# Hybrid decoder trunk, one core: the first quarter's scale on the chip instead of through DRAM, and the second quarter's embedding moved to the last heads

## The chip, the core and the metric

The kernel runs on one core of a Trainium2 chip. Its engines are TensorE (PE in the profile, with PEld for the loading of weights), VectorE (DVE), ScalarE (ACT), GpSimd (POOL) and SyncE (SP), which issues all the transfers of this kernel. Each engine works off its own instructions in order and waits on semaphores for the others. The metric is the device time of one execution in microseconds (us). Before the change the median of three runs was 2870.23 us (2867.57 to 2871.44); the profiled execution, which all the rows below come from, took 2865.62 us.

## What is computed

One layer over 2048 tokens of width 1024, in float32:

```python
hn   = rms_norm(x, pre_mix_norm)
proj = hn @ w_in                       # 1024 -> 32 blocks of 128, and 8 columns for decay and beta
o_a  = gated DeltaNet, 4 heads of 128  # short conv, l2norm, chunked delta rule, gated head norm
o_b  = HGRN2, 4 heads of 128           # lower-bounded forget gate, chunked, gated head norm
h    = x + rms_norm(concat(o_a, o_b) @ w_out, post_mix_norm)
y    = square(relu(rms_norm(h, pre_mlp_norm) @ w_mlp_up)) @ w_mlp_down     # width 4096
h    = h + rms_norm(y, post_mlp_norm)
e    = rms_norm(p @ w_ple_proj, ple_norm)                                  # p has width 256
out  = h + e * sigmoid(h @ w_ple_gate)
```

`rms_norm(x, w)` is `x * rsqrt(mean(x * x) + 1e-6) * w` over the 1024 columns of a token.

## The kernel before, in words

**Tiling.** The tokens are worked in four quarters of 512 (`QT`). Activations lie transposed, features on the 128 partitions and tokens along the free dimension, so a 1024-wide operand is eight tiles of 128x512. A matrix product splits each operand into a high and a low part (`split`: ACT rounds a copy to fp32r, VectorE subtracts), and takes three matmuls per 128 features: high by high, high by low, low by high. A block of 128 output columns over 1024 features is thus 24 matmuls of 128x512; an embedding tile, over the 256 features of p, is six.

**Stages.** A first stage (pool `es`) embeds quarters of p and prepares the first quarter of x. Then, for each quarter, the mixers: first `mm_ab`, the projection of the eight decay and beta columns, then four heads, each with eight projections (`works`, line 910 on). Last come the output projection, the MLP and the gated addition of e.

**Order.** The PE's instructions stand in the order in which the program writes them (`manual_schedule`); in the first stage and through the mixers this holds for SP too. On the other engines a scheduler orders the instructions by its own estimate of the time. The mixers use a clock of ticks: a projection of 24 matmuls is three ticks of eight, and generators such as `gdn_mixer`, `decays` and `norm_steps` are put into an agenda (`at`) so that each of their steps is issued at a given tick. An engine that waits holds up all that stands behind it in its queue, and this goes for SP's transfers too.

**The first stage (lines 349 to 396).** It loads the weights of the embedding (`plea0`, `plea1`), two quarters of p (`praw`), the first quarter of x by rows (`xs`, 2 MB), constants, and the first quarter of x transposed (`xraw`, 2 MB). ACT squares the rows of x with a sum per row; VectorE and POOL turn the sums into scales, four per partition. `spread` stores these to DRAM as a row and `spread_load` loads the row back to all partitions. `operand` then scales a tile of `xraw` and splits it into the ring pool `ra` (ten buffers). In between, sixteen calls of `embed_tile` embed the two quarters: six matmuls, a copy `e` by ACT that is stored to `ed`, a square by ACT, and an addition by VectorE into `acc_e`.

**The first head's chain.** After `mm_ab`, `decays` (line 448) computes the decays on ACT and VectorE, sums them with scans into `gb`, stores them (`gd`) and has PE transpose them (`ps_gb`). `gdn_mixer` loads them back (`gf_g`), forms a lower triangular matrix (`u_g`), stores and reloads it in another layout (`ud_g`, `sys_g`), and VectorE solves it in 31 steps of a product and a reduction (lines 615 and 616). The result goes through DRAM once more (`xd_g`, `xx_g`) and PE uses it from `psp_g` (line 638) on. The tiles `bound`, `um`, `S` and `gb` take over the room of the pool `es`, so their memsets wait for the last store of an `e`.

**The buffers of the weights.** In the pool `wp` (line 438 on) raw weights have two buffers and split ones three. A split weight is also stored to a DRAM cache (`keep`), so its buffer comes free only when PE has used it and that store has landed. Loads, splits and stores run two to three projections ahead.

**The last heads (lines 939 to 977).** When all projections are done, the mixers of the last head still have steps to run. Between these, the embeddings of the third and fourth quarter fill PE, one tile per tick (`fill`), and then the first two tiles of the output projection (`first_outs`, `mmo`). Their copies `e` use two buffers ("ld" of the pool `m2`), which the raw tiles of p share.

Of the kernel before, what the change touches and what calls it, by code (L numbers as in the profile page):

```python
# [77 lines left out]
def trunk(ctx, tc, x, xT, pT, vecs, w_in, w_ab, gdn_a_log, gdn_dt_bias, w_out, w_up, w_down,  # L78
# [39 lines left out]
    def col(r):  # L118
        return cols[:, r : r + 1]
# [10 lines left out]
    def vectors():  # L130

        ps = bank("ps_rows", pp)
        PE.transpose(ps[:, :N_ROWS], rows, ident[:N_ROWS, :N_ROWS])
        V.tensor_copy(cols, ps[:, :N_ROWS])
        V.tensor_scalar(gate_w, cols[:, R_GNORM : R_HNORM + 1], 0.5, None, ALU.mult)
# [141 lines left out]
    def stage_ple(i, name):  # L277
# [5 lines left out]
        def ready(eng):  # L283
            w = wp.tile([P, 2, KD, P], F32R, tag="whl", name=f"w_{name}")
            for half in range(2):
                sl = slice(half * KD // 2, (half + 1) * KD // 2)
                split(w[:, :, sl], eng, raw[:, sl])
            return w
# [15 lines left out]
    x_r, xts, accs = {}, {0: []}, {0: None, 1: None}  # L304
# [44 lines left out]
    with ExitStack() as ectx:  # L349
        es = ectx.enter_context(tc.tile_pool(name="es", bufs=1))  # L350
        with tc.manual_schedule(engines={mybir.EngineType.SP}):
            ple0 = stage_ple(0, "plea0")
            praw = [es.tile([P, 2, QT], F32, name=f"praw{q}") for q in range(2)]
            nc.sync.dma_start(praw[0], pT[:, tok(0)].rearrange("(k p) t -> p k t", p=P))
            rows4 = x[tok(0), :].rearrange("(p c) d -> p c d", c=NC)
            xs = es.tile([P, NC, D], F32, name="xs")
            for c in range(0, NC, 2):
                nc.sync.dma_start(xs[:, c : c + 2], rows4[:, c : c + 2])
            nc.sync.dma_start(ident, consts[:, C_IDENT])
            nc.sync.dma_start(rows, vecs)  # L360
            nc.sync.dma_start(dec[:, 0:1], gdn_a_log.rearrange("o h -> h o"))
            nc.sync.dma_start(dec[:, 1:2], gdn_dt_bias.rearrange("o h -> h o"))
            nc.sync.dma_start(praw[1], pT[:, tok(1)].rearrange("(k p) t -> p k t", p=P))
            ple1 = stage_ple(1, "plea1")
# [6 lines left out]
            ple = [ple0(V), None]  # L371
            pts = [[operand(ra, None, f"pT{q}_{k}", raw=praw[q][:, k]) for k in range(2)] for q in range(1)]
            ss = sm.tile([P, NC], F32, tag="ss", name="ss_x0")
            for c in range(NC):
                S.activation(xs[:, c], xs[:, c], AF.Square, accum_out=ss[:, c : c + 1])
            V.tensor_scalar(ss, ss, 1.0 / D, EPS, ALU.mult, ALU.add)
            rsqrt(ss)
            stores = []
            for d in range(4):
                stores.append(embed_tile(0, d, ple[0], pts[0], accs, es, 6))  # L380
                if d == 1:
                    vectors()
            pts.append([operand(ra, None, f"pT1_{k}", raw=praw[1][:, k]) for k in range(2)])
            ple[1] = ple1(V)
            x_r[0] = spread(ss, "x0")
            rsb = spread_load(x_r[0], "x0")
            for d, q in [(d, 1) for d in range(4)] + [(d, q) for d in range(4, KD) for q in range(2)]:
                stores.append(embed_tile(q, d, ple[d // 4], pts[q], accs, es, 6))
                stores.pop(0)()
                if len(xts[0]) < KD:  # L390
                    k = len(xts[0])
                    xts[0].append(operand(ra, None, f"xt0_{k}", col(R_PREMIX + k), rsb, raw=xraw[:, k]))
            for f in stores:
                f()


    with mixers as mctx:
# [36 lines left out]

        def stage(name, src, k=KD):

            raw = wp.tile([P, k, P], F32, tag="raw", name=f"raw_{name}", bufs=2)
            nc.sync.dma_start(raw, src)

            def ready():  # L440
                w = wp.tile([P, 2, k, P], F32R, tag="whl", name=f"w_{name}")
                split(w, V, raw)
                return w

            return ready
# [378 lines left out]
        staged, split_w = {}, {}  # L824
# [81 lines left out]
        for q in range(2):  # L906
            at(0, norm_steps(accs[q], 1.0 / D, EPS, f"e{q}", partial(ple_r.__setitem__, q)),
               [4 * q + i for i in (0, 2, 4, 5)])
        with tc.manual_schedule(engines={mybir.EngineType.SP}):
            stage_work(0)  # L910
            stage_work(1)
            split_work(0)
            stage_work(2)
            split_work(1)
            for j, (name, key, src, q, h, then, g, b) in enumerate(works):
# [9 lines left out]
                for s in range(SPT):  # L925
                    for i in range(s * nt // SPT, (s + 1) * nt // SPT):
                        PE.matmul(ps, *terms[i], start=i == 0, stop=i == nt - 1)  # L927
# [7 lines left out]
            qs = (2, 3)  # L935
            ple = [stage_ple(i, f"pleb{i}") for i in range(2)]
            pts = {q: [operand(ra, pT[blk(k), tok(q)], f"pT{q}_{k}", stage=m2) for k in range(2)] for q in qs}
# [3 lines left out]
            at(clock[0], mix_operands(0), (1, 2, 3, 4, 6, 7, 9, 11))  # L941
# [3 lines left out]
            call(clock[0] + 13, partial(ready_out, 1))  # L945
            call(clock[0] + 14, partial(stage_out, 2))
# [693 lines left out]
```

## Time and profile before

| | |
|---|---|
| median of three runs | 2870.23 us |
| the profiled execution, its span | 2865.62 us, 2863.8 us |
| PE, PEld busy | 97%, 80% |
| DVE, ACT, POOL busy | 75%, 46%, 4% |
| read from and written to HBM | 420.14 MB, 166.92 MB |
| first matmul of mm_ab | 46.09 us after the start |
| third tile of the output projection | from 1245.56 us |

In a row of the timeline the first number is the start and the second the time, in us; then engine, line of the kernel, operation, output <- inputs, shapes and count; in brackets stands the idle time of the engine ahead of it and who ended it. `SPq` is a transfer being issued, not its landing. In a group of the list by line stand the count, the busy time in us, the mean of one in ns, and the idle time before. A window lists the busy time of PE, PEld, DVE, ACT and POOL, the granted clock of PE as a share, the share of the DMA engines and GB/s.

### The profile page before, as it was taken

What the parts mean: (1) busy time and instruction counts of PE and PEld (TensorE: products, weight loads), DVE (VectorE), ACT (ScalarE), POOL (GpSimd) and SP (SyncE); (2) the same over time, 40 slices, a digit from 0 to 9 for tenths busy, and PEclk for the clock granted to TensorE, in tenths of its full rate; (3) what the DMA queues carried; (4) which work ended last, traced back from release to release, by engine and by line L of the source; (5) the groups of instructions that cost most, each with busy time, mean ns of one, the idle gap of its engine ahead of it and who ended that gap; (6) DMA issues with size and microseconds to landing.
All of it is one profiled execution on the core that took longest, in us unless ns stands there. A gap on an engine that the chain in (4) does not pass through costs nothing.

```text
span 2863.8 us, 39544 instructions
## 1 busy us (share of the span) xinstructions
PE 2773.0 (97%) x13361; PEld 2293.7 (80%) x13361; DVE 2158.2 (75%) x4712; ACT 1331.2 (46%) x2460; POOL 108.7 (4%) x104
## 2 busy tenths in 40 slices
PE   7899999999999999999989999999999999999999
PEld 5688788888888888777768887888888888887887
DVE  6688787887878887758887886776787765567675
ACT  6354334333333333457555655554555445465431
POOL 0000000000000000000000000000100000001000
PEclk9999999999999999999999999999999999999999
DMA  7666667655665666587755646666564446577573
GB/s 254 223 222 205 215 213 246 201 199 201 224 195 190 212 199 196 159 284 247 258 173 192 229 166 209 217 212 210 193 210 139 148 157 213 188 255 239 196 230 116
DMA packets 268602, 589.70 MB, mean 206 GB/s; under 512 B 55642, under 2 KB 59960, under 8 KB 249072
## 3 DMA queue, kind: packets, MB, share of 16 engines
q1 hardware_dynamic: 268400, 587.18, 61.5%
q8 instruction: 106, 1.74, 0.3%
q14 instruction: 96, 0.79, 0.1%
HBM read 420.14 MB, written 166.92 MB: 205 GB/s over the span
## 4 chain that ended last, share of the span: by engine, by line
PE 46%; DVE 3%; DMA 3%; issue 2%; ACT 2%; POOL 0%; SPq 0%; DVEq 0%; ACTq 0%; POOLq 0%
PE u L996 21%; PE d L996 18%; PE mmg L996 6%; DMA da<-sumd 1%; DMA raw_out<-in_w_out_dram 1%; DMA xo<-in_xT_dram 1%; DMA b<-h1d 0%; PE mmo L996 0%; DVE w_out L162 0%; DVE t L162 0%; ACT L1033 0%; ACT L1032 0%; ACT w_out L161 0%; DVE b L1143 0%; POOL acc_y L225 0%
## 5 line engine op out<-in xcount | busy, mean ns | idle before, releaser
L927 PE MATMUL mm<-xt,w 128*128 128x512 f32 x3072 | 791.2, 405 | 2.6 <-ACT w L161 1.2
L927 PEld LDWEIGHTS mm<-xt,w 128*128 128x128 f32 x3072 | 564.6, 191 | 122.8 <-ACT w L161 1.6
L996 PE MATMUL d<-db,da 128*128 128x512 f32 x2688 | 613.0, 390 | 4.2 <-DVE db L215 3.2
L996 PE MATMUL u<-t,wu 128*128 128x512 f32 x2604 | 603.4, 393 | 3.3 <-ACT wu L161 3.2
L996 PEld LDWEIGHTS d<-db,da 128*128 128x128 f32 x2688 | 504.0, 188 | 112.6 <-DVE db L215 5.8
L996 PEld LDWEIGHTS u<-t,wu 128*128 128x128 f32 x2604 | 488.8, 188 | 117.2 <-ACT wu L161 4.1
L215 DVE TENSOR_TENSOR db<-db 128x512 fp32r<-128x512 f32 x224 | 160.8, 718 | 69.9 <-ACT db L214 69.4
L1325 DVE TENSOR_TENSOR u<-u,u 128x512 f32<-128x512 f32 x224 | 150.8, 684 | 72.1 <-PE u L996 71.0
L996 PE MATMUL mmo<-mixT,w_out 128*128 128x512 f32 x720 | 171.5, 398 | 9.1 <-DVE w_out L162 6.8
L214 ACT ACTIVATE db<-db 128x512 fp32r<-128x512 f32 x224 | 140.9, 629 | 78.7 <-DMA db<-hid 76.3
L996 PE MATMUL mmg<-h2T,wg 128*128 128x512 f32 x768 | 177.5, 393 | 0.0
L996 PEld LDWEIGHTS mmo<-mixT,w_out 128*128 128x128 f32 x720 | 137.0, 191 | 42.6 <-DVE w_out L162 8.5
L996 PEld LDWEIGHTS mmg<-h2T,wg 128*128 128x128 f32 x768 | 144.2, 188 | 32.8
L1366 ACT ACTIVATE u<-u 128x512 f32<-128x512 f32 x128 | 80.9, 632 | 179.6 <-DVE u L1325 179.2
L162 DVE TENSOR_TENSOR da<-da 128x512 fp32r<-128x512 f32 x128 | 94.3, 737 | 91.0 <-ACT da L161 90.5
L615 DVE TENSOR_TENSOR pr_g<-xs_g,sys_g 128x4 f32<-128x4 f32 (+30 forms) x496 | 136.1, 274 | 29.3 <-DMA sys_g<-ud_g 19.3
L161 ACT ACTIVATE da<-da 128x512 fp32r<-128x512 f32 x128 | 80.5, 629 | 140.0 <-DMA da<-sumd 117.3
L616 DVE TENSOR_REDUCE xs_g<-pr_g 128x4 f32<-128x8 f32 (+30 forms) x496 | 111.0, 224 | 9.8
L161 ACT ACTIVATE wu<-a 128x512 fp32r<-128x512 f32 x124 | 73.9, 622 | 46.7 <-DMA a<-in_w_up_dram 44.6
L225 POOL TENSOR_TENSOR acc_y<-acc_y,sq_y 128x512 f32<-128x512 f32 x28 | 38.7, 1382 | 1389.4 <-ACT sq_y L224 1389.4
L162 DVE TENSOR_TENSOR wu<-a,wu 128x512 fp32r<-128x512 f32 x124 | 84.9, 688 | 4.0 <-ACT wu L161 4.0
L726 PE MATMUL at_h<-q_h,k_h 128*128 128x64 f32 x640 | 82.6, 273 | 3.2 <-DVE tail_g L548 1.7
(364 smaller groups left out, 3893.1 us busy)
## 6 DMA issues: line engine op xcount, KB each, us to landing
w<-cache_in SPq DMA_DIRECT2D x96, 1024.0 KB
db<-hid SPq DMA_DIRECT2D x224, 256.0 KB
cache_in<-w SPq DMA_DIRECT2D x32, 1024.0 KB
hid<-u SPq DMA_DIRECT2D x128, 256.0 KB
da<-sumd SPq DMA_DIRECT2D x128, 256.0 KB
a<-in_w_up_dram SPq DMA_DIRECT2D x124, 256.0 KB
hid<-ht SPq DMA_DIRECT2D x96, 256.0 KB
dr<-in_w_down_dram SPq DMA_DIRECT2D x96, 256.0 KB
```

Of the source, the lines that this page charges most:

```text
L161: S.activation(t[:, 0], raw, AF.Copy)
L162: eng.tensor_tensor(t[:, 1], raw, t[:, 0], ALU.subtract)
L214: S.activation(t[:, 0], plain(t), AF.Copy)
L215: V.tensor_tensor(t[:, 1], plain(t), t[:, 0], ALU.subtract)
L225: eng.tensor_tensor(acc, acc, sq, ALU.add)
L615: V.tensor_tensor(pr[:, :, 0:i], xs[:, :, 0:i], sys[:, None, 0:i, i].broadcast_to([P, GC, i]), ALU.mult)
L616: V.tensor_reduce(xs[:, :, i], pr[:, :, 0 : i + 1], AX.X, ALU.add)
L726: PE.matmul(ps[:, c, :], k[:, blk(c)], odd, start=True, stop=True)
L927: PE.matmul(ps, *terms[i], start=i == 0, stop=i == nt - 1)
L996: PE.matmul(ps, a, b, start=start, stop=stop)
L1325: V.tensor_tensor(c[new], c[old], ps, ALU.add)
L1366: S.activation(c[k], c[k], AF.Relu)
```

## The change

In the first stage the rows of x are no longer loaded. ACT squares the transposed tiles two at a time and VectorE adds them up; four matmuls of one column each sum over the partitions, with the tokens on the partitions of the result. The scales, four per partition as before, multiply the identity matrix into a diagonal, and one matmul with all ones gives the row of scales on all partitions, in PSUM (`rs_x0`), where the scaling of x reads it. ACT and VectorE now follow the written order in this stage, as SP does: scalings run one tile ahead of the splits, and copies of embedding tiles stand at chosen places between them. The first two weights of the projections are loaded and the first is split here as well (`stage` is moved up unchanged). The e tiles are stored after the scalings, their squares are kept in pairs and added at the end, followed by `vectors()`.

Only the first quarter of p is embedded here. The second joins the third and fourth in the last heads, so `fill` has 24 tiles; p of a later quarter is loaded when the seventh tile of the quarter before is issued. The ticks of the output projection's first operands and weights, of the first norm of e and of the first decays' transposes are moved.

```diff
@@ first stage
-        with tc.manual_schedule(engines={mybir.EngineType.SP}):
+        first = {mybir.EngineType.SP, mybir.EngineType.Activation, mybir.EngineType.DVE}
+        with tc.manual_schedule(engines=first):
             ple0 = stage_ple(0, "plea0")
-            praw = [es.tile([P, 2, QT], F32, name=f"praw{q}") for q in range(2)]
-            nc.sync.dma_start(praw[0], pT[:, tok(0)].rearrange("(k p) t -> p k t", p=P))
-            rows4 = x[tok(0), :].rearrange("(p c) d -> p c d", c=NC)
-            xs = es.tile([P, NC, D], F32, name="xs")
-            for c in range(0, NC, 2):
-                nc.sync.dma_start(xs[:, c : c + 2], rows4[:, c : c + 2])
...
+            def put(d):
+                if d % 2 == 0:
+                    es_sq[d // 2] = es.tile([P, 2, QT], F32, name=f"esq{d // 2}")
+                e = es.tile([P, QT], F32, tag="ld", name=f"e0_{d}", bufs=KD)
+                S.activation(e, sums[d], AF.Copy)
+                S.activation(es_sq[d // 2][:, d % 2], sums.pop(d), AF.Square)
+                puts.append((ed[0][d], e))
...
+            def x_squares(k):
+                if k == 0:
+                    S.activation(total, xraw[:, :2], AF.Square)
+                else:
+                    sq = es.tile([P, 2, QT], F32, tag="xsq", name=f"xsq{k}", bufs=2)
+                    S.activation(sq, xraw[:, k : k + 2], AF.Square)
+                    V.tensor_tensor(total, total, sq, ALU.add)
...
+            columns_of_rows()
+            ps = bank("ss_x0", po)
+            for c in range(NC):
+                PE.matmul(ps[:, c : c + 1], acc[:, blk(c)], one[:, 0:1], start=True, stop=True)
+            ss = sm.tile([P, NC], F32, tag="ss", name="ss_x0")
+            V.tensor_scalar(ss, ps[:, :NC], 1.0 / D, EPS, ALU.mult, ALU.add)
+            rsqrt(ss)
+            ple[1] = ple1(V)
+            put(2)
+            diag = es.tile([P, NC, P], F32, name="xdiag")
+            V.tensor_tensor(diag, over_chunks(ident), ss[:, :, None].broadcast_to([P, NC, P]), ALU.mult)
+            rsb = bank("rs_x0", po)
+            embed(4)
+            PE.matmul(rsb, one, diag.rearrange("p c n -> p (c n)"), start=True, stop=True)
+            put(3)
+            split_w = {0: ab_ready()}
+            w0_ready = stage("4_0_0", w_in[4])
+            for d in range(5, KD):
+                embed(d)
...
+            scaled(0)
+            for k in range(KD):
+                scaled(k + 1)
+                xts[0].append(operand(ra, None, f"xt0_{k}", raw=raws[k]))
+                if k in (1, 3, 5, 6):
+                    put({1: 4, 3: 5, 5: 6, 6: 7}[k])
             nc.sync.dma_start(cst[:, C_NEG:], consts[:, C_NEG:])
...
-            x_r[0] = spread(ss, "x0")
-            rsb = spread_load(x_r[0], "x0")
-            for d, q in [(d, 1) for d in range(4)] + [(d, q) for d in range(4, KD) for q in range(2)]:
-                stores.append(embed_tile(q, d, ple[d // 4], pts[q], accs, es, 6))
-                stores.pop(0)()
...
+            for a in puts:
+                nc.sync.dma_start(*a)
+            vectors()
+            pair = es_sq[0]
+            for i in range(1, KD // 2):
+                V.tensor_tensor(pair, pair, es_sq[i], ALU.add)
+            accs[0] = st.tile([P, QT], F32, tag="acc", name="acc_e0", bufs=3)
+            V.tensor_tensor(accs[0], pair[:, 0], pair[:, 1], ALU.add)
@@ mixers
-        for q in range(2):
-            at(0, norm_steps(accs[q], 1.0 / D, EPS, f"e{q}", partial(ple_r.__setitem__, q)),
-               [4 * q + i for i in (0, 2, 4, 5)])
+        at(0, norm_steps(accs[0], 1.0 / D, EPS, "e0", partial(ple_r.__setitem__, 0)), (7, 9, 11, 13))
...
-                            at(clock[0], decays(ps, q), (0, 2, 4, 5))
+                            at(clock[0], decays(ps, q), (0, 2, 5, 6) if q == 0 else (0, 2, 4, 5))
@@ last heads
-            qs = (2, 3)
+            qs = (1, 2, 3)
...
-            at(clock[0], mix_operands(0), (1, 2, 3, 4, 6, 7, 9, 11))
+            at(clock[0], mix_operands(0), (9, 10, 11, 12, 14, 15, 18, 19))
...
-            call(clock[0] + 13, partial(ready_out, 1))
-            call(clock[0] + 14, partial(stage_out, 2))
+            call(clock[0] + 21, partial(ready_out, 1))
+            call(clock[0] + 22, partial(stage_out, 2))
...
+                    if d == KD - 2 and q + 1 in qs:
+                        store()
+                        store = None
+                        pts[q + 1] = load_p(q + 1)
```

More of the change, by code (lines that the diff above doesn't have):

```diff
@@ L287, in ready, with stage @@
                 split(w[:, :, sl], eng, raw[:, sl])
+                if half == 0 and then is not None:
+                    then()
+            return w
+        return ready
+    def stage(name, src, k=KD):
+        raw = wp.tile([P, k, P], F32, tag="raw", name=f"raw_{name}", bufs=2)
+        nc.sync.dma_start(raw, src)
+        def ready():
+            w = wp.tile([P, 2, k, P], F32R, tag="whl", name=f"w_{name}")
+            split(w, V, raw)
             return w
@@ L433, in x_scale @@
             x_r[q] = spread(ss, f"x{q}")
[L435 to L445, printed above, removed]
         def decays(ps, q):
```

75 lines of the change are left out of this document (41 added, 34 removed).

## The prediction

> **What bounds the kernel now.** First the head of the page, then the windows, then the timeline at the two places that the change touches.
>
> ```profile
> span 2863.8 us, 39544 instructions
> PE 2773.0 (97%) x13361; PEld 2293.7 (80%) x13361; DVE 2158.2 (75%) x4712; ACT 1331.2 (46%) x2460; POOL 108.7 (4%) x104
> ```
>
> PE is busy for 97% of the span, so what counts is where the other 3% lies, and what a moved matmul costs where it arrives. The windows (PE, PEld, DVE, ACT and POOL busy, then granted clock) show the first 140 us to be the loosest part:
>
> ```profile
> 20.00:40.00 20.00, 13.11 (x47) 9.55 (x46) 14.89 (x23) 13.70 (x24) 0.00 (x0) 0.83 0.79 279
> 120.00:140.00 20.00, 9.35 (x42) 7.99 (x41) 10.96 (x32) 5.11 (x12) 0.00 (x0) 0.74 0.41 133
> 140.00:160.00 20.00, 20.00 (x128) 17.75 (x127) 16.01 (x38) 12.71 (x34) 1.01 (x1) 1.00 0.84 298
> ```
>
> PE had 13.11 of 20 us to do just ahead of the first projection and 9.35 of 20 between 120 and 140; from 140 on it is full. The timeline says why the first hole is there:
>
> ```profile
> 24.09 0.33 SPq L236 DMA_DIRECT2D rsb_x<-rd_x  x1
> 28.02 2.08 DVE L203 SCALAR_TENSOR_TENSOR xraw<-xraw,cols,rsb_x 128x512 f32<-128x512 f32 x3 [0.71 <-DMA rsb_x<-rd_x]
> 46.09 5.87 PE L927 MATMUL mm_ab<-xt,w_ab 128*128 128x512 f32 x24 [0.31 <-ACT sq_e L224]
> 52.26 7.62 PE L927 MATMUL mm<-xt,w 128*128 128x512 f32 x32
> ```
>
> The scales of x make a trip through DRAM: they are loaded back at 24.09, and the first scaling starts at 28.02. The decay projection mm_ab starts at 46.09, after 96 embedding matmuls; the next group starts at 52.26, or 51.8 without the two norm matmuls before it. From the last row, a 128x512 matmul costs (7.62 - 0.40) / 31 = 0.233 us.
>
> The second hole belongs to the first head's solve. Its chain runs from the decays' scans to psp_g:
>
> ```profile
> 60.49 1.35 DVE L462 TENSOR_TENSOR_SCAN gb<-one,sp 4x128 f32<-4x128 f32 x4
> 60.95 1.19 PE L470 MATMUL ps_gb<-cst,gb 36*128 36x36 f32 x4 [0.61 <-DVE gb L462]
> 85.25 3.94 SPq L605 DMA_DIRECT2D ud_g<-u_g  x4
> 98.16 0.17 DVE L615 TENSOR_TENSOR pr_g<-xs_g,sys_g 128x4 f32<-128x4 f32 x1 [3.25 <-DMA sys_g<-ud_g]
> 127.42 0.28 DVE L616 TENSOR_REDUCE xs_g<-pr_g 128x4 f32<-128x128 f32 x1
> 132.77 2.05 PE L638 MATMUL psp_g<-xx_g,um 128*128 128x128 f32 x8 [10.65 <-DVE xx_g L630]
> ```
>
> Scans end at 61.84; u_g is stored at 85.25; VectorE starts the solve at 98.16 and ends it at 127.70; PE waits 10.65 us and restarts at 132.77. So this stage is set by a VectorE and DMA chain. A lead that PE wins before it is kept only as far as this chain gains it too.
>
> **The change, front part.** It removes the 2 MB load of x, its four ACT passes, the row's DRAM trip and 48 matmuls of the second quarter. It adds squares over the transposed x, four one-column matmuls, a diagonal, and one all-ones matmul that leaves the scale in PSUM. SP, ACT and VectorE now run in the written order.
>
> ```profile
> 4.91 1.15 ACT L161 ACTIVATE w_plea<-raw_plea 128x512 fp32r<-128x512 f32 x2 [2.89 <-DMA raw_plea<-in_w_ple_dram]
> 7.06 1.15 ACT L161 ACTIVATE pT<-praw 128x512 fp32r<-128x512 f32 x2 [1.00 <-DMA praw<-in_pT_dram]
> 9.55 1.06 ACT L375 ACTIVATE xs<-xs 128x1024 f32<-128x1024 f32 x1 [1.34 <-DMA xs<-in_x_dram]
> 10.52 0.18 ACT L375 ACTIVATION_READ_ACCUMULATOR xs<-xs 128x1 f32 x1
> ```
>
> Arrivals: plea at 4.91, pT at 7.06, a further megabyte by 9.55, so 2.5 us per MB. The four parts of xraw, now third in the SP queue, land at about 8.3, 9.6, 10.9 and 12.1, before ACT needs them. ACT in its new order: pT and the second half of plea from 7.06 to 8.7, first squares to 9.7, then e and its square for tile 0 (whose matmuls wait for pT's split) to 11.5, two squares to 13.4, e and square of tile 1 to 14.4, last squares to 15.4 (0.97 each, the distance of the start of one xs pass to its read-out).
>
> ```profile
> L203 DVE SCALAR_TENSOR_TENSOR xraw<-xraw,cols,rsb_x 128x512 f32<-128x512 f32 x8 | 5.7, 748 | 0.7 <-DMA rsb_x<-rd_x 0.7
> L162 DVE TENSOR_TENSOR xt<-xraw,xt 128x512 fp32r<-128x512 f32 x8 | 5.3, 687 | 0.2 <-ACT xt L161 0.2
> L162 DVE TENSOR_TENSOR w<-raw,w 128x1024 fp32r<-128x1024 f32 x2 | 2.4, 1222 | 0.7 <-ACT w L161 0.7
> L157 POOL TENSOR_TENSOR ss_x<-ss_x,mhalf 128x4 f32<-128x4 f32 x1 | 1.0, 1022 | 15.1 <-DVE ss_x L376 15.1
> ```
>
> After that: VectorE add 1.15 and 0.6 (17.3); column matmuls and hand-over, a new operation, estimated at 1.0 (18.4); scale 0.2; POOL 1.02 and hand-overs (19.9); diagonal 0.7 (20.6); the all-ones matmul, in f32, also new, estimated at 1.0 (21.7). Neither form is in the trace; between 0.3 (one short pass) and 2 (half clock, below) each, they move the next number by 1.4 less or 2 more. VectorE splits w_ab meanwhile. The first scaling starts at about 22.5 with hand-overs, against 28.02. From there VectorE paces: eight scalings at 0.67 (0.75 less overlap), eight splits at 0.61, one weight split at 1.15: 11.4 us, the last operand at 34.2. The group behind mm_ab can start at 34.8: **17.0 us ahead** of 51.8. The new work costs nothing beyond this, since it is the path already counted.
>
> Now what is late next. VectorE leaves the last operand with a backlog that lay elsewhere before: the constants of vectors() with the split of weight 2 (2.5), three 1024-wide adds and one 512-wide of squares (4.05), and the memsets of um, S and gb (2.6, from 51.56 to 54.2 below), which still stand behind the es pool's last store.
>
> ```profile
> 51.56 1.03 DVE L412 MEMSET um<- 128x512 f32 x2
> 53.76 0.48 DVE L453 MEMSET gb<- 36x512 f32 x1
> 79.74 0.43 SPq L177 DMA_DIRECT2D cache_in<-w  x1
> 87.02 1.06 ACT L161 ACTIVATE w<-raw 128x1024 fp32r<-128x1024 f32 x1 [1.43 <-DMA cache_in<-w]
> ```
>
> That is 34.2 + 9.15 = 43.4 for the end of gb's memset, against 54.2 (53.76 + 0.48): 10.8 ahead. ACT agrees: the split of weight 3 stands ahead of the decays' first activation in its new order and needs w_ab's slot, so the store of w_ab must land. Such a store took 79.74 to 87.02, 7.3 us; issued at about 34.1 behind the load of weight 3, it frees ACT at about 41.5 and the decays start at about 43. From the memset to the end of the scans took 61.84 - 54.2 = 7.6 us; one more weight split on both engines now lies in between, 9.6. Scans end at 53.0, **only 8.8 ahead**. PE reaches ps_gb after mm_ab, 24 and 16 matmuls: 34.8 + 40 x 0.233 = 44.1. It waits about 9 us, where it waited 0.61. The decay step moved by one tick buys 1.9 us of that. Queued behind ps_gb are the rest of that projection and all others.
>
> ```profile
> 122.00:124.00 2.00, 0.12 (x1) 0.00 (x0) 2.00 (x7) 0.00 (x0) 0.00 (x0) 1.00 0.00 0
> 128.00:130.00 2.00, 0.00 (x0) 0.00 (x0) 0.17 (x1) 0.16 (x1) 0.00 (x0) 0.50 0.11 33
> 136.00:138.00 2.00, 2.00 (x7) 1.69 (x8) 1.10 (x3) 0.00 (x0) 0.00 (x0) 0.64 0.99 343
> ```
>
> An idle stretch also costs clock: after 122.1 PE idles, the clock stands at 0.50 from 128 and is back during 136 to 138, so some 4 us at half speed, 2 us of work. [...]
>
> PE's lead behind ps_gb is 8.8 + 1.9 - 0.5 (a norm that went elsewhere) - 2 = 8. On the SP queue the lead of u_g's store is larger: gd goes out at 53.1, weights 5 to 8 follow as the slots' stores land (7.3 each), with the norm's load and row store once in between; added up, u_g's store leaves at 71.4, 13.9 ahead of 85.25. The solve's VectorE steps alternate with work that needs the next head's projections, so its end lies between a lead of 8 and one of 13.9; nearest to PE's, since the steps alternate in one queue: **9.5 us gained at psp_g** (ends 6, if the scaling starts 3 us late, and 17, if nothing is held up).
>
> **The change, last heads.** The second quarter's eight tiles come first there, then the third's and fourth's.
>
> ```profile
> 1156.60 12.79 SPq L201 DMA_DIRECT2D raw_pT<-in_pT_dram  x4
> 1230.21 2.02 PE L956 MATMUL mmo<-mixT,w_out 128*128 128x512 f32 x8
> 1238.02 0.49 PE L667 MATMUL psb_g<-r_g,xx_g 128*128 128x128 f32 x2 [1.16 <-DVE r_g L664]
> 1245.56 34.23 PE L996 MATMUL mmo<-mixT,w_out 128*128 128x512 f32 x146
> ```
>
> Before, both quarters' pT were loaded at 1156.60, well ahead. mmo starts at 1230.21, and its third tile at 1245.56; from there PE has no hole to 1280, so every microsecond of delay at 1245.56 is one of the kernel. Added: 48 matmuls x 0.233 = 11.2 and a norm pair that was in front, 0.46, less 1.16, the psb_g wait that goes: +10.5, the lower bound.
>
> Then the loads. pT of the next quarter is issued at the seventh tile, into the two "ld" buffers of e tiles: so store e, wait for its landing, load, split, then the matmul two tiles on.
>
> ```profile
> 1229.44 0.38 SPq L299 DMA_DIRECT2D ed<-e  x1
> 1233.16 0.60 ACT L297 ACTIVATE e<-mme 128x512 f32<-128x512 f32 x1 [2.16 <-DMA ed<-e]
> 1196.04 4.44 DMA mixT<-mixd
> ```
>
> A store issued at 1229.44 let the e two tiles on start at 1233.16: 3.7 us. A 256 KB load took 4.44. Going from third to fourth quarter: e5's store at 1229.4, e6's 0.5 later, loads at 1233.2 and 1233.7, landed at 1237.6 and 1238, split 0.6, against a need at 1230.2. That is 8 us of waiting by these rows; some of w_out's loads and stores now come later in the queue, so the stretch is less crowded, and I take 5.5. [...] The first transition falls where PE waits for the last head's solve in any case; 0.5.
>
> From there on each e needs the store of two tiles before to land, with the last head's small loads between the stores on SP: (0.6 + 3.7 + 0.6) / 2 = 2.45 us per tile where PE needs about 1.8; half of it shows over eight tiles, 2.5. Half clock after the wait: 1.
>
> ```profile
> 1245.09 0.40 PE L261 MATMUL nrm_g<-hl_g,ones 128*128 128x512 f32 x1
> 1243.44 1.17 SPq L328 DMA_DIRECT2D raw_out<-in_w_out_dram  x2
> 1268.55 0.32 SPq L532 DMA_DIRECT2D mixd<-og_g  x1
> ```
>
> Weights: the fifth w_out load was issued at 1243.44, ahead of the last norm (1245.09); in the new queue it stands behind the store of og_g, 23.5 us after that norm (1268.55). With less in between it lands some 24 us after it, and PE wants it 24.3 after; 0 to 4, taken as 1. Sum here: 10.5 + 5.5 + 0.5 + 2.5 + 1 + 1 = **+21** (ends 10.5 and 28).
>
> **Sum.** 21 - 9.5 = +11.5 on the profiled run's 2865.6, that is 2877. The three runs shown have a median of 2870.2, 4.6 above it; on that footing 2881.
>
> **Rivals.** *The transfers land sooner* (20%): with less traffic in both places the two pT waits shrink to 1 and the stores keep up: the last heads cost 12 to 13; front 9.5 to 11. About 2872, no change. For it: DMA moves 2 MB less at the start; against it: 3.7 and 4.44.
>
> *The solve's hole closes* (18%, faster): the 10.65 us before psp_g are the largest reserve. If VectorE, no longer fed with the second quarter's squares, lets the decays out at 46 or earlier, PE's whole lead of 17 holds and psp_g starts before 113, 20 ahead; the last heads at 13 then give 2863. It decides for "faster" once psp_g's lead exceeds the last heads' cost by 6. Against it: the 9 us of backlog counted above.
>
> *The stores set the pace* (7%): if all sixteen later tiles go at 2.45 to 2.7 and the fifth w_out load is 4 late, the last heads cost 28 to 31: 2890.
>
> **How the numbers follow.** My forecast, both waits about as reckoned, has 55%: 2875 to 2889 by itself. With the rivals to both sides 2862 to 2893 should hold the time 8 times in 10. No change means within 0.2%, 5.7 us, about what the runs can tell apart: the second rival and a sliver of the first give faster 0.19, the rest of the first and the forecast's lower edge the same 0.22, what is left slower 0.59.
>
> **What would show it.** Right: mm_ab's matmuls done by about 35; PE idle for 7 to 10 us ahead of ps_gb, released by VectorE's gb; psp_g between 119 and 126; in the last heads a PE wait of 4 to 8 us, released by pT, ahead of the fourth quarter's first tile, and w_out's third tile about 9 to 14 us later than 1245.56. Wrong: ps_gb without a wait, or psp_g before 115; no wait on pT; the scaling not begun by 26.

## The result, and the profile after

The changed kernel took 2887.74 us (median of four runs, 2885.58 to 2890.97) against 2870.84 for the kernel before, measured beside it (2867.57 to 2871.96). The ratio is 1.0066, with a 95% interval of 1.0054 to 1.0078: slower by about 17 to 19 us. The profiled execution took 2887.92 us, close to its kernel's median. The one of before took 2865.62, 5 us under its own, so the two traces lie 22.3 us apart and some 5 of these are not the change's.

First the busy times of the engines and three windows of the changed kernel (PE, PEld, DVE, ACT and POOL busy, granted clock, DMA share, GB/s).

```profile
PE 2789.1 (97%) x13371; PEld 2304.5 (80%) x13371; DVE 2163.8 (75%) x4714; ACT 1328.8 (46%) x2456; POOL 107.4 (4%) x104
...
40.00:60.00 20.00, 14.19 (x51) 10.44 (x50) 16.86 (x39) 10.95 (x16) 0.52 (x1) 0.83 0.43 163
48.00:50.00 2.00, 2.00 (x6) 1.61 (x5) 1.61 (x3) 1.87 (x2) 0.00 (x0) 0.50 0.00 0
100.00:120.00 20.00, 8.82 (x43) 6.96 (x41) 16.11 (x45) 5.62 (x9) 0.00 (x0) 0.81 0.27 92
```

The hole that lay between 120 and 140 us now lies between 100 and 120, and a new one has opened between 40 and 60. The timeline of the same kernel shows both, and how the front runs:

```profile
23.04 1.41 DVE L446 SCALAR_TENSOR_TENSOR xraw<-xraw,cols,rs_x 128x512 f32<-128x512 f32 x2 [1.03 <-PE rs_x L436]
35.17 5.77 PE L978 MATMUL mm<-xt,w 128*128 128x512 f32 x24
42.75 1.06 ACT L163 ACTIVATE w<-raw 128x1024 fp32r<-128x1024 f32 x1 [7.29 <-DMA cache_ab<-w_ab]
44.38 0.48 DVE L509 MEMSET gb<- 36x512 f32 x1
46.13 6.16 PE L978 MATMUL mm<-xt,w 128*128 128x512 f32 x16 [5.19 <-ACT gb L510]
52.25 1.35 DVE L518 TENSOR_TENSOR_SCAN gb<-one,sp 4x128 f32<-4x128 f32 x4
52.71 1.19 PE L526 MATMUL ps_gb<-cst,gb 36*128 36x36 f32 x4 [0.42 <-DVE gb L518]
74.75 3.13 SPq L661 DMA_DIRECT2D ud_g<-u_g  x4
86.82 0.17 DVE L671 TENSOR_TENSOR pr_g<-xs_g,sys_g 128x4 f32<-128x4 f32 x1 [3.42 <-DMA sys_g<-ud_g]
121.71 2.05 PE L694 MATMUL psp_g<-xx_g,um 128*128 128x128 f32 x8 [12.88 <-DVE xx_g L686]
```

The first scaling is 5.0 us earlier than before (28.02), the projection behind mm_ab 16.6 us (51.8), but the scans end only 8.2 us earlier (53.6 against 61.84) and psp_g 11.1 us (132.77). PE stands idle for 5.19 us ahead of the second projection, because ACT has not yet read mm_ab out of the bank that this projection needs: ACT had itself waited 7.29 us for the store of w_ab, and VectorE reached the memset of gb only at 44.38. PE then runs 16 matmuls in 6.16 us instead of 3.7, at half clock (0.50 from 48 to 50).

Next the last heads: rows of the same kernel's timeline, three short windows that show the clock, and two long ones. Each long window runs from one landmark of the work to the next: first embedding tile, third tile of the output projection, its first norm. Then come the windows of the kernel before between the same landmarks:

```profile
1228.03 3.23 PE L190 MATMUL mme<-pT,w_pleb 128*128 128x512 f32 x6 [6.65 <-ACT pT L163]
1244.34 1.93 PE L190 MATMUL mme<-pT,w_pleb 128*128 128x512 f32 x6 [3.47 <-ACT sq_e L226]
1262.42 11.36 PE L1055 MATMUL mmo<-mixT,w_out 128*128 128x512 f32 x48
1269.12 0.90 SPq L344 DMA_DIRECT2D raw_out<-in_w_out_dram  x2
1275.84 0.88 PE L1055 MATMUL mmo<-mixT,w_out 128*128 128x512 f32 x2 [2.06 <-ACT w_out L163]
1202.00:1204.00 2.00, 2.00 (x9) 1.81 (x9) 0.65 (x2) 1.40 (x3) 0.00 (x0) 0.50 0.40 138
1228.00:1230.00 2.00, 1.97 (x4) 1.35 (x5) 1.53 (x3) 1.72 (x3) 0.00 (x0) 0.50 0.36 139
1246.00:1248.00 2.00, 2.00 (x5) 1.12 (x4) 1.91 (x5) 1.37 (x3) 0.60 (x1) 0.50 1.06 434
1170.19:1262.42 92.23, 77.15 (x374) 61.94 (x374) 54.08 (x112) 50.55 (x94) 7.57 (x7) 0.91 0.54 178
1262.42:1310.24 47.82, 44.94 (x186) 35.22 (x184) 22.38 (x30) 23.80 (x38) 1.01 (x1) 0.96 0.89 310
```
```profile
1179.30:1245.56 66.26, 58.89 (x326) 49.47 (x324) 46.11 (x100) 38.76 (x71) 5.49 (x5) 0.97 0.64 210
1245.56:1288.97 43.41, 43.13 (x186) 34.38 (x184) 21.48 (x29) 22.84 (x37) 2.02 (x2) 1.00 0.85 292
```

From the first embedding tile to the third tile of the output projection it was 66.26 us and is now 92.23: 26.0 more. PE is busy for 18.3 us of these: 50 matmuls added make 11.7, so 6.6 us are matmuls run slowly, at a granted clock of 0.91 on the mean. The other 7.7 us are added waits. The next stretch, up to the first norm of the output projection, costs 4.4 us more, with a wait for a weight that was issued at 1269.12. PE entered the last heads 9.1 us ahead, leaves this second stretch 21.3 us behind, and ends 22.3 behind.

### The profile page after: what moved, and what is told of

Its sections match the earlier page's. It is cut to its first block, busy times and chain, and to the rows that moved or that the text cites. A ratio compares the mean times of both kernels' runs of the same rounds, so it can differ in the third digit from the quotient of the medians.

```text
span 2886.1 us, 39570 instructions
## 1 busy us (share of the span) xinstructions
PE 2789.1 (97%) x13371; PEld 2304.5 (80%) x13371; DVE 2163.8 (75%) x4714; ACT 1328.8 (46%) x2456; POOL 107.4 (4%) x104
## 4 chain that ended last, share of the span: by engine, by line
PE 45%; DVE 4%; issue 3%; DMA 3%; ACT 2%; POOL 0%; SPq 0%; DVEq 0%; ACTq 0%; POOLq 0%
PE u L1055 21%; PE d L1055 17%; PE mmg L1055 6%; PE mmo L1055 1%; DMA da<-sumd 1%; DMA xo<-in_xT_dram 0%; DMA raw_out<-in_w_out_dram 0%; DMA dr<-in_w_down_dram 0%; DVE w_out L164 0%; DVE t L164 0%; ACT L1092 0%; DMA b<-h1d 0%; ACT L1091 0%; DVE b L1202 0%; ACT w_out L163 0%
```

## The experiments

All ratios are to the kernel before, measured beside each run; its medians there were 2869.04 to 2870.26 us.

**The two halves apart.** The first run takes the changed front alone:

```diff
-            qs = (1, 2, 3)
+            qs = (2, 3)
...
-            at(clock[0], mix_operands(0), (9, 10, 11, 12, 14, 15, 18, 19))
+            at(clock[0], mix_operands(0), (1, 2, 3, 4, 6, 7, 9, 11))
...
...
+            ed[1], ple_r[1] = ed[2], ple_r[2]
```

> The changed front without the changed last heads: the second quarter's embedding is left out altogether (its 48 matmuls run nowhere; the third quarter's e and norm stand in for the second's), and the last heads are those of before. Theory: the front is worth what PE's lead shows at the first embedding tile of the last heads in the two traces, 1179.30 - 1170.19 = 9.1 us, and nothing gives it back: 2870.8 - 9 = about 2862 (2858 to 2865), psp_g near 121.7. Rival: the lead is eaten up before the end, since later stages are paced by transfers that do not start earlier: 2868 to 2872.

Measured: 0.9969 (0.9960 to 0.9979), median 2861.17. The second puts the changed last heads on the kernel before, whose front stays as it is:

```diff
-            qs = (2, 3)
+            qs = (1, 2, 3)
...
+                    if d == KD - 2 and q + 1 in qs:
+                        store()
+                        store = None
+                        pts[q + 1] = load_p(q + 1)
...
```

> The kernel before with the changed last heads alone: the second quarter is embedded twice, in the front as before and again in the last heads as changed. Theory: the two parts are independent, so this costs what the traces show from the first embedding tile to the first norm of the output projection, about 26 us in the last heads and 4.4 us in the waits for w_out behind them: 2870.8 + 30 = about 2900 (2896 to 2904). Rival: the last heads cost so much only because the changed front lets PE arrive earlier than its transfers; then this costs little more than the whole change, 2886 to 2892.

Measured: 1.0103 (1.0089 to 1.0117), median 2898.92. The product of the two ratios is 1.0072, the whole change 1.0066: within the intervals the halves add up to it. With the front of before, the last heads show the same waits at the same places, so the early arrival of PE is not what makes them:

```profile
1242.27 3.23 PE L188 MATMUL mme<-pT,w_pleb 128*128 128x512 f32 x6 [6.81 <-ACT pT L161]
1259.09 2.93 PE L188 MATMUL mme<-pT,w_pleb 128*128 128x512 f32 x6 [3.33 <-ACT sq_e L224]
1291.58 0.94 PE L1004 MATMUL mmo<-mixT,w_out 128*128 128x512 f32 x2 [3.37 <-ACT w_out L161]
1185.50:1276.85 91.35, 75.59 (x375) 60.70 (x374) 54.09 (x112) 50.57 (x94) 7.57 (x7) 0.91 0.53 175
```

These rows are of the last heads alone. Its first embedding tile starts near 1185.5, where before has 1179.30, with psp_g of the first head at 133.15 and 132.77: the mixers in between differ by some 6 us from one trace to the next, and a lead of one trace over another at that place is no better known than that.

**The waits of the last heads.** p of all three quarters is loaded ahead of the first tile:

```diff
-            pts = {1: load_p(1)}
+            pts = {q: load_p(q) for q in qs}
...
-                    if d == KD - 2 and q + 1 in qs:
-                        store()
-                        store = None
-                        pts[q + 1] = load_p(q + 1)
```

> The changed kernel with p of all three later quarters loaded and split ahead of the first tile, as the kernel before did with its two. Theory: the waits for pT (6.65 us at 1228.03, 1.03 and 0.25 us at 1200) go, and with them the half clock behind them, some 4 us: 10 to 13 us less than 2887.7, 2875 to 2878. Rival: the two buffers of e set the pace of all tiles once pT does not, so the wait comes back ahead of the next e: 3 us less at most, 2884 to 2888.

Measured: 1.0034 (1.0022 to 1.0046), median 2878.38, 9.4 us under the changed kernel's, just short of the 10 to 13 of the first theory: the waits for pT and what follows them cost about 9 us. On top of this the next run adds a third buffer for e and moves w_out's loads ahead:

```diff
-                    new = embed_tile(q, d, ple[d // 4], pts[q], accs, m2, 2)
+                    new = embed_tile(q, d, ple[d // 4], pts[q], accs, m2, 2, "rsx" if len(fill) % 3 == 0 else "ld")
...
-            call(clock[0] + 22, partial(stage_out, 2))
+            call(clock[0] + 8, partial(stage_out, 2))
+            call(clock[0] + 22, partial(stage_out, 3))
+            call(clock[0] + 25, partial(ready_out, 2))
+            call(clock[0] + 26, partial(stage_out, 4))
...
```

> The changed kernel with p loaded ahead, a third buffer for e (room of the scale row that is idle there), and the loads of w_out's third to fifth block and the split of the third put ahead of the last steps of the last head. Theory: of the 18.6 us that the last heads still cost with p ahead, the waits for sq_e (2.38 and 2.90 us, set by the stores of e), the half clock behind them (2.5) and the waits for w_out (2.8) go, and some 11 us, the bare matmuls, stay: 2869 to 2872, no gain over before. Rival: the stores share SP's queue with loads that wait for their own sources, and the weights come no sooner: 2875 to 2879.

Measured: 1.0020 (1.0010 to 1.0029), median 2874.64, between the two theories. The windows and the wait that is left, first with p ahead, then with all three:

```profile
1238.88 2.93 PE L190 MATMUL mme<-pT,w_pleb 128*128 128x512 f32 x6 [2.90 <-ACT sq_e L226]
1173.90:1256.70 82.80, 72.74 (x375) 59.48 (x374) 53.38 (x114) 49.68 (x93) 8.08 (x7) 0.96 0.56 185
```
```profile
1262.88 0.90 SPq L344 DMA_DIRECT2D raw_out<-in_w_out_dram  x2
1269.39 29.16 PE L1057 MATMUL mmo<-mixT,w_out 128*128 128x512 f32 x112 [4.33 <-ACT w_out L163]
1171.10:1248.10 77.00, 70.80 (x375) 58.21 (x374) 53.13 (x113) 49.00 (x91) 7.34 (x7) 0.98 0.60 198
1248.10:1298.40 50.30, 45.93 (x186) 36.15 (x185) 22.63 (x30) 24.08 (x38) 1.23 (x2) 0.93 0.83 291
```

The last heads went from 92.23 to 82.80 to 77.00 us, the last 10.7 above the 66.26 of before: PE is busy for 11.9 us more, the added matmuls, and waits 1.2 us less. But the output projection, reached earlier, then waits 4.33 us for the next weight, whose load still goes out at 1262.88, so a part comes back. Even with no more waiting in the last heads than before, the embedding costs its full matmul time there.

**What bounds the front.** The store of w_ab goes out early, and in the second run three additions are left out too:

```diff
             split_w = {0: ab_ready()}
             w0_ready = stage("4_0_0", w_in[4])
+            keep("ab", split_w[0])
...
-            for i in range(1, KD // 2):
-                V.tensor_tensor(pair, pair, es_sq[i], ALU.add)
...
```

> The changed kernel with the store of w_ab to its cache issued right after its split instead of at 34.36. ACT then does not wait 7.29 us for w_ab's buffer at 42.75. Theory: VectorE's backlog (vectors, additions, memsets to 44.86) sets the decays all the same, so the wait ahead of the second projection still ends at about 46 and the time stays: 2886 to 2889. Rival: ACT's wait sets it, and the second projection's matmuls start 3 us or more earlier: 2882 to 2885.

> As the run with the early store of w_ab, and three of the four additions of the squares of the first quarter's e left out (3.72 us of VectorE; that quarter's norm is then taken over two tiles). Theory: with both bounds gone the memset of gb ends near 41, the second projection restarts at about 42 instead of 46.13, scans end about 49, and psp_g follows by 3 to 4 us: 2883 to 2885. Rival: psp_g is set by the transfers of u_g and by the solve's own order, and moves less than 1 us: 2886 to 2889.

Measured: 1.0053 (1.0036 to 1.0071), median 2886.14, and 1.0042 (1.0027 to 1.0058), median 2885.00. Both intervals overlap the changed kernel's own, so the times alone tell little; the traces do. The early store alone, then with the additions left out:

```profile
44.45 0.48 DVE L510 MEMSET gb<- 36x512 f32 x1
45.60 5.36 PE L980 MATMUL mm<-xt,w 128*128 128x512 f32 x16 [4.17 <-ACT gb L511]
120.40 2.05 PE L695 MATMUL psp_g<-xx_g,um 128*128 128x128 f32 x8 [13.16 <-DVE xx_g L687]
```
```profile
42.24 0.48 DVE L508 MEMSET gb<- 36x512 f32 x1
43.40 3.99 PE L978 MATMUL mm<-xt,w 128*128 128x512 f32 x16 [1.72 <-ACT gb L509]
116.92 2.05 PE L693 MATMUL psp_g<-xx_g,um 128*128 128x128 f32 x8 [12.64 <-DVE xx_g L685]
```

The early store did not move gb's memset (44.45 against 44.38), but it shortened PE's wait from 5.19 to 4.17 us and brought psp_g 1.3 us forward. With 3.72 us less on VectorE as well the memset came 2.1 us earlier, the wait fell to 1.72, and psp_g came 4.8 us earlier than in the changed kernel. So VectorE's backlog sets the larger part of this chain and the store a smaller one; no run leaves out the additions alone, so what they are worth without the early store is not shown. That the gain at psp_g shows so little in the time stays open; it is within the spread of the mixers behind it.

**Which part of the front earns.** The kernel before, with only the second quarter's embedding left out of its front:

```diff
...
-            for d, q in [(d, 1) for d in range(4)] + [(d, q) for d in range(4, KD) for q in range(2)]:
-                stores.append(embed_tile(q, d, ple[d // 4], pts[q], accs, es, 6))
-                stores.pop(0)()
+            for d in range(4, 4 + KD):
+                if d < KD:
+                    stores.append(embed_tile(0, d, ple[d // 4], pts[0], accs, es, 6))
+                    stores.pop(0)()
...
```

> The kernel before without the second quarter's embedding in the front and nothing else changed (its 48 matmuls run nowhere; the third quarter's e and norm stand in for the second's): scales of x by rows and through DRAM as before. With the run of the changed front alone it parts the front's gain in two. Theory: leaving out the second quarter's work on PE, ACT and VectorE carries most of it, since the chain of the decays and of the solve starts behind VectorE's backlog, which shrinks here by eight additions, eight copies and the split of p; the new scale then adds 2 to 4 us of the 8.9: 2863 to 2866. Rival: the first scaling at 28.02, behind the trip through DRAM, holds everything, so leaving out matmuls ahead of it is worth little: 2868 to 2871.

Measured: 0.9957 (0.9944 to 0.9969), median 2856.92. This missed both: with the scales by way of DRAM the front without the second quarter is not slower than the new one but, by the ratios, some 3 us faster (their intervals overlap). To see whether the new scale's work or its order is at fault:

```diff
-        first = {mybir.EngineType.SP, mybir.EngineType.Activation, mybir.EngineType.DVE}
+        first = {mybir.EngineType.SP}
```

> The changed front alone (second quarter's embedding left out, last heads of before, as in the earlier run), but with ACT and VectorE in the first stage ordered by the scheduler again and only SP written out. Theory: what the new scale loses against the old one (2861.2 to 2856.9) is VectorE work that it adds, the sums of x's squares and the diagonal, some 5 us up to the decays; the order of the queues does not matter: 2859 to 2863. Rival: the written order loses it, since it puts constants and additions behind the last operand; then this comes to 2855 to 2858.

Measured: 0.9958 (0.9946 to 0.9971), median 2857.66. The theory fell, and the time lies in the rival's range: with ACT and VectorE left to the scheduler the new scale equals the old one. That the written order costs the other 3 us is likely but not shown, since the intervals of 0.9969 and 0.9958 overlap. The three fronts, changed, with the free order, and with the old scale:

```profile
50.70 1.35 DVE L518 TENSOR_TENSOR_SCAN gb<-one,sp 4x128 f32<-4x128 f32 x4
121.59 2.04 PE L694 MATMUL psp_g<-xx_g,um 128*128 128x128 f32 x8 [14.12 <-DVE xx_g L686]
```
```profile
49.55 1.35 DVE L518 TENSOR_TENSOR_SCAN gb<-one,sp 4x128 f32<-4x128 f32 x4
119.31 2.05 PE L694 MATMUL psp_g<-xx_g,um 128*128 128x128 f32 x8 [13.36 <-DVE xx_g L686]
```
```profile
26.02 2.08 DVE L203 SCALAR_TENSOR_TENSOR xraw<-xraw,cols,rsb_x 128x512 f32<-128x512 f32 x3
49.53 1.36 DVE L461 TENSOR_TENSOR_SCAN gb<-one,sp 4x128 f32<-4x128 f32 x4
117.49 2.05 PE L637 MATMUL psp_g<-xx_g,um 128*128 128x128 f32 x8 [6.92 <-DVE xx_g L629]
```

The old scale begins scaling at 26.02, about 3 us behind the new one, and its scans begin at 49.53, no later than either. It adds up the squares of e between other steps of VectorE, and ACT sums the squares of x for it; the new front gives VectorE the sums of x and puts the constants and the sums of e behind the last operand.

**The embedding in the solve's hole.** If it is the move out of the front that earns and the last heads that cost, the second quarter may go where PE waits for psp_g. It is made two projections between the first two heads, with the first head's later steps six ticks later, the changed front and the last heads of before:

```diff
...
+                if (q, h) == (0, 0):
+                    a_steps, b_steps = ([o + PLUS * (o >= 24) for o in s] for s in (a_steps, b_steps))
+                    works += [(f"plec{i}", "ple", i, 0, None, None, None, None) for i in range(2)]
...
```

> The changed front, the last heads of before, and the second quarter's embedding as two projections between the first and the second head, with the first head's later steps six ticks later, so that its 11.2 us of matmuls stand where PE waited 12.88 us for psp_g. Squares are added up by POOL. Theory: the idle time ahead of psp_g is filled by nearly its whole length, and the rest is as in the front alone: 2861 to 2866. Rival: the copies and splits that come with the embedding hold up VectorE's and ACT's chain through the solve, and psp_g starts 5 to 10 us later: 2867 to 2873.

Measured: 0.9994 (0.9984 to 1.0003), median 2867.83, 6.7 us above the front alone and in the rival's range. psp_g started at 133.08, 11.5 us later than with the front alone, and PE had waited 3.47 and 3.43 us for p on the way. Loading p earlier:

```diff
-        call(3 + 18, load_second)
+        call(3 + 6, load_second)
```

> As the kernel with the embedding between the first two heads, but the second quarter's p is loaded and split twelve ticks earlier, ahead of the solve. There PE waited 3.47 and 3.43 us for the split of p, behind weights on ACT and behind the solve's steps on VectorE, then ran some 3 us at half clock, and the stores of e held the solve's own store back on SP to 121.19. Theory: these go, psp_g starts at 123 to 126 instead of 133.08, and the time is 7 to 10 us below that kernel's 2867.8: 2858 to 2862. Rival: the 11.2 us of matmuls that PE now does in time only move the wait to the end of the solve, which the additions on POOL stretch (a VectorE step beside one took 1.43 us instead of 0.35); then psp_g starts at 128 to 131: 2864 to 2867.

Measured: 0.9990 (0.9979 to 1.0001), median 2869.26, with psp_g at 131.97: behind both expectations. The waits for p went, and another took their place (SP, ACT and PE in the timeline of this run):

```profile
102.08 0.33 SPq L299 DMA_DIRECT2D raw<-in_w_in_dram  x1
102.47 6.10 SPq L997 DMA_DIRECT2D ed<-e  x3
106.67 1.06 ACT L163 ACTIVATE w<-raw 128x1024 fp32r<-128x1024 f32 x1 [4.56 <-DMA raw<-in_w_in_dram]
108.76 1.65 PE L190 MATMUL mme<-pT,w_plec 128*128 128x512 f32 x3 [7.74 <-ACT sq_e L226]
```

A load that waited for its buffer stood ahead of the stores of e on SP, and the split of that load ahead of e's copy on ACT. The next run embeds before it splits and loads:

```diff
+                if key == "ple":
+                    embed_second(src, split_w.pop(j))
                 split_work(j + 2)
                 stage_work(j + 3)
+                if key == "ple":
+                    continue
                 keep_work(j)
-                if key == "ple":
-                    embed_second(src, split_w.pop(j))
-                    continue
```

> As the kernel with the embedding between the first two heads and p loaded early, but the next projections' weights are split and loaded behind each half of the embedding instead of ahead of it. There PE waited 7.74 us ahead of the fifth tile: on ACT two splits of weights stood ahead of the copy of e, the second until its load had landed, and on SP that load stood ahead of the stores of e. Theory: this wait and the half clock behind it go, the embedding ends near 107 instead of 117, and the time is 5 to 9 us lower than that kernel's 2869.3: 2860 to 2864. Rival: the solve ends at 115 in any case, and its result reaches PE 10 us or more later, so PE waits for psp_g instead: 2866 to 2870.

Measured: 0.9995 (0.9986 to 1.0004), median 2868.86. The wait fell to 3.42 us, but the time did not follow:

```profile
103.40 1.39 PE L190 MATMUL mme<-pT,w_plec 128*128 128x512 f32 x3 [3.42 <-ACT sq_e L226]
128.55 1.16 PE L694 MATMUL psp_g<-xx_g,um 128*128 128x128 f32 x8 [1.33 <-DVE xx_g L686]
```

The time lies in the rival's range, but its mechanism shows only in part: PE waits for the solve's result again, for 1.33 us, and psp_g starts 3.4 us earlier than in the run before (131.97). Why the time did not follow is open. Last, the same embedding behind the front of before:

> The whole computation: the front of before without the second quarter (scales through DRAM, scheduler's order), that quarter's embedding between the first two heads in the order of the last such run, the last heads of before. Theory: the embedding costs there what it cost behind the changed front, 6 to 8 us over the run without it: 2856.9 + 7 = 2863 to 2866, 0.15 to 0.25 per cent faster than the kernel before. Rival: with this front PE waits only 6.92 us for psp_g, so less of the 11.2 us is hidden and the time is that of before, 2867 to 2871.

Its edit is the three diffs above put on the kernel with the old scale. Measured: 1.0020 (1.0012 to 1.0029), median 2875.61, with runs from 2868.94 to 2879.32; worse than both expectations. Its profiled run is the fastest of them, so the trace does not show where the slower ones lose, and this stays open. No version here is measurably faster than the kernel before with the whole computation.

## Why the prediction was right

The forecast was 2881, slower, with 2875 to 2889 for its own case; 2887.74 lies in it, near the top. Both halves came out with the sign reckoned, one nearly to size and one too small. Two of the signs named did not come as written: PE's idle time was to stand ahead of ps_gb, where only 0.42 us was left, and w_out's third tile was to come 9 to 14 us later and came 16.9 us later. It is in part by the width of the range that the time lies in it: the last heads cost 30.4 us where the sum had 21, and that is the size of the third rival (28 to 31, 2890 in all), though not its mechanism.

**Front, the scaling and mm_ab: right.** First scaling 22.5 forecast, 23.04 measured; the group behind mm_ab 34.8 and 35.17. The two new matmul steps, taken at 1.0 us each with no row behind them, took 1.05 (17.41, the column sums) and 2.07 (20.93, the all-ones product). (22.5 and 11.4 make 33.9, not the 34.2 given for the last operand; its split ended at 34.5.)

**Front, what is late next: right in the chain, wrong in the place of the wait.** The end of gb's memset was put at 43.4 and came at 44.86, the scans at 53.0 and 53.6. The wait was expected ahead of ps_gb, 9 us; it stood one projection earlier, 5.19 us, since the second projection needs the bank that ACT has still to read mm_ab from, and only 0.42 us was left at ps_gb. With 2.4 us of half clock behind it that is 8.0, against 9 and 2. Of the two causes named side by side both bear on it: the early store took 1.0 us off the wait, the shorter VectorE list on top of it 2.5 more.

**Front, the gain at psp_g: right in size, in part by luck.** 9.5 us was forecast; it is 11.1 between the traces, and the front alone with 0.9969 gains 6 to 11.5 us. PE's lead behind ps_gb was 8.2 us, as reckoned, but it had grown to 13.3 at the last projection ahead of the wait (started at 102.97 against 116.28). The lead of u_g's store was 10.5 us, not 13.9, and the solve started 11.3 us earlier (86.82 against 98.16). So the chain of the solve set psp_g, and not PE's lead, near which the forecast had put it.

**Front, where the gain comes from: right that the 17 us are not kept, but the prediction did not see that none of the gain is the scale's.** It costed the part as one lead to be kept or lost. The runs put the whole gain on the second quarter's absence (0.9957 without any other change); the new scale adds nothing to it, and its written order may take some 3 to 4 us away.

**Last heads, the matmuls: right.** 10.5 was the lower bound, and the run with p ahead, a third buffer and earlier weights came to 10.7 in that stretch.

**Last heads, the waits: the mechanisms right, the sizes too small.** These are the terms that were mis-sized: 21 forecast, 30.4 measured (26.0 and 4.4). The pT wait ahead of the fourth quarter was 6.65 for 5.5 taken, between that and the 8 of the rows. The stores of e, 2.5, showed as one wait of 3.47. The first transition, taken as hidden at 0.5, showed 1.03 and 0.25 us of waits: the last head's solve did not cover it. Half clock was charged 1 us, the author's estimate from the one hole of before (at 0.50 from 128 to 136), and the slow matmuls measure 6.6, because it follows all three of these waits and not only one: the clock stood at 0.50 in the windows behind each. By the rows behind the three waits, some 5 of the 6.6 us are theirs (an estimate); the rest is not placed. Behind the 6.65 us wait one tile took 3.23 us where 1.65 is usual; behind the first transition, with waits of only 1.03 and 0.25 us, a tile took 2.23 (at 1203.30) and the clock stood at 0.50 from 1202 to 1204. How long a wait must be to cost clock is not shown. The late w_out load, taken as 1 of 0 to 4, cost 4.4 with its slow matmuls; the mechanism was the one named, a load behind the store of og_g (1267.58, the load at 1269.12).

**The rivals.** *Transfers land sooner* did not happen: the pT wait was 6.65 us, not 1. *The solve's hole closes* did not: PE waits 12.88 us there instead of 10.65. *The stores set the pace* is partly what is seen: one wait of 3.47 us for sq_e in the last quarter, not a slower pace over all sixteen tiles, and a w_out load that cost 4.4 us, about the 4 that it named. Its size fits better than its mechanism.

**Footing.** The forecast stood on the median, 4.6 above the profiled run of before; on that run's own footing the 11.5 us would have ended at 2877, further from 2887.74.

## What to carry to other kernels

A start made earlier is worth what the queue behind it allows: list what each engine has yet to do between the early event and the one that sets the pace, and ask first whether simply leaving out work there would do the same; here it did all of it. Work moved from a stage with slack into one where PE is full cost its whole time here, 11.7 us of matmuls, and the waits that came with it were charged again at half clock (0.50 behind each of the three, some 5 us of slow matmuls by the estimate above), so count waits, not only their length. On SP a load that waited for its buffer held up the stores of e behind it, and PE waited 7.74 us, so filling a hole is a question of three queues and not of PE's alone.

## What was not expected of the hardware

Products of the solve on VectorE took 1.04 to 1.44 us beside an addition on POOL, where 0.33 to 0.39 is usual, though neither waited for the other's data. In the run that embeds before it splits, POOL's and VectorE's rows of the same stretch are:

```profile
110.16 1.34 POOL L227 TENSOR_TENSOR acc_e<-acc_e,sq_e 128x512 f32<-128x512 f32 x1 [0.71 <-ACT sq_e L226]
...
110.00 0.34 DVE L671 TENSOR_TENSOR pr_g<-xs_g,sys_g 128x108 f32<-128x108 f32 x1
110.38 0.27 DVE L672 TENSOR_REDUCE xs_g<-pr_g 128x4 f32<-128x112 f32 x1
110.68 1.05 DVE L671 TENSOR_TENSOR pr_g<-xs_g,sys_g 128x112 f32<-128x112 f32 x1
...
112.08 0.36 DVE L671 TENSOR_TENSOR pr_g<-xs_g,sys_g 128x116 f32<-128x116 f32 x1
```

The product that began at 110.68, while POOL's addition ran from 110.16 to 111.50, took 1.05 us; the ones on either side took 0.34 and 0.36. The reduction at 110.38 ran at its usual 0.27. The slow product ended 0.23 us after the addition. So it was with five of the solve's products, two in this run and three in the run with p loaded early: each began during an addition, took 1.04 to 1.44 us where its neighbours took 0.33 to 0.39, and ended 0.22 to 0.25 us after the addition. What holds such a product up is not shown. So additions given to an idle POOL were not free, some 0.7 to 1.1 us each to the solve's chain (an estimate from these times); no run separates this from the rest of the embedding's price there.

In the changed kernel the clock also fell after short waits of PE. After 2.06 us of idling (the row of 1275.84) windows of 0.5 us show it at 0.50 from 1276.5 to 1279.5 and at 1.00 from 1280; after 0.92 us, at 1172.77, it stayed at 1.00 (1172 to 1175).
